# Layer 1's keys and values in one written order, between two layers of a fp32 transformer block on one core

## The chip, the cores and the metric

The kernel runs on one core of a Trainium2 chip. The metric is the device time of one execution in microseconds (us), the median of several runs; lower is better. A core has a matrix engine (TensorE, PE in the rows; its weight loads are shown apart as PEld), three engines for element-wise work (VectorE or DVE, ScalarE or ACT, GpSimd or POOL) and SyncE (SP), whose queue here issues the transfers between the core's memory and HBM. Each engine works through its own queue in order and waits on semaphores for the others.

## The reference

Two layers run over 1024 latent tokens and 256 context tokens of width 1024, all in fp32. Layer 0 is grouped-query attention, layer 1 multi-head latent attention. What the change touches lies at the border: layer 0's output projection with its gated residual, layer 1's norm and modulation, and layer 1's keys and values, which are made from a 256-wide compressed row and a 32-wide rotary key:

```python
x = x + gate[:, None, :] * y            # y = (o * silu(g)) @ w_out; likewise ctx with gate_c
h  = rms_norm(x, norm_w) * (1.0 + scale[:, None, :]) + shift[:, None, :]
hc = rms_norm(ctx, norm_w) * (1.0 + scale_c) + shift_c
...
kv = (rms_norm(kv_a, p["kv_a_norm"]) @ p["w_kv_b"]).reshape(B, n, MLA_HEADS, MLA_NOPE + MLA_V)
k_nope, v = jnp.split(kv, [MLA_NOPE], axis=-1)
return rms_norm(k_nope, p["k_nope_norm"]), rms_norm(k_r, p["k_rope_norm"]), v
```

## The kernel before, in words

Tokens come in ten tiles of 128 rows, tiles 0 to 7 latent and 8 and 9 context. A product of fp32 matrices is three matmuls per 128 rows of depth: each operand is split into a high part (a cast to a shorter format, ACT) and a low part (what is left, DVE or POOL), and `mm3` (lines 88 to 97) adds hi·hi, hi·lo and lo·hi in PSUM. Weights come from HBM into one of three buffers tagged `wraw` (`load_weight`, the cast in line 156, the subtraction in line 135), and the two parts go to a pair `wa`, `wb`, of which the ring has two. The raw rows of the attention's result (`oraw`) use the same three buffers.

At the end of layer 0, `out_proj` takes a tile at a time: the rows are split into `oh`, `ol`, 2 x 24 matmuls make `y` (the two halves of the output width use one weight pair each), DVE multiplies by the gate (`yt`), DVE and POOL add to the residual `xt`. `sink0` then stores latent tiles to `x1d` (a row of SP) and normalises `xt` in place: sum of squares on ACT (`junk`), mean on DVE, power of -1/2 on POOL (`x_rs`), scale on DVE (line 257). Since the scale writes in place, it has to wait until the store to `x1d` has read the tile. `modulate` turns a pair of normalised tiles by 16 transposes on PE (line 269), applies scale and shift (`hmod`, DVE), and splits into `hh` and `hl`. It is called one tile after the pair is complete; the context pair is modulated right behind `out_proj`.

Layer 1's keys and values are a software pipeline by `staged`: for a tile, compress (24 matmuls of 128x288, `mm`, lines 1280 to 1303), latent (3 transposes, split into `kvh` and `kvl`), expand (four groups of 6 matmuls of 128x512, `mmk` and `mmv`, for two halves of the heads; squares on ACT, `kss` and `kn_ms` on DVE, `kn_rs` on POOL, `kn` on DVE in line 1322; `v` copied out by ACT) and store (2 x 4 transposes of `kn`, `th` on ACT, `tl` on DVE, transfers). All products of this stage share four PSUM buffers. Only DVE is held to the written order there; the order of the other engines is chosen by the scheduler when the kernel is built. Then comes the q stage, whose compress step has 24 matmuls of 128x384 a tile.

Of the kernel before, what the change touches and what calls it, by code (L numbers as in the profile page):

```python
# [35 lines left out]
def hybrid_kernel(ctx: ExitStack, tc: tile.TileContext, ins: dict, out: bass.AP):  # L36
# [569 lines left out]
    def out_proj(l, ws, resid, sink, nt, op, xp, gp, ps_y, first, started, by_half):  # L606
# [24 lines left out]
        def mult(t, ks, first, last):  # L631
            oh, ol, xt, ys = t
            for n in range(2):
# [4 lines left out]
        def add(tt, t):  # L638
            oh, ol, xt, ys = t
            cond = 0 if tt < TL else 1  # L640
            for n in range(2):
                ns = slice(n * 512, (n + 1) * 512)
                yt = op.tile([P, 512], F32, name="yt", tag="yt")
# [550 lines left out]

    with ExitStack() as st:
        xp = st.enter_context(tc.tile_pool(name="xpp0", bufs=4, **right))
        gp = st.enter_context(tc.tile_pool(name="gp0", bufs=1, **right))
        wk = st.enter_context(tc.tile_pool(name="wk1a", bufs=3, **right))
# [14 lines left out]
        def sink0(tt, xt):  # L1213
# [17 lines left out]
        out_proj(0, wo, resid0, sink0, TT, op, xp, gp, ps_mm, first, started0, False)  # L1231
        stO.close()
        hT1.append(alloc_hT(stc, "hctx1", NC))
        flush(1)
# [11 lines left out]
    def bcast(tab, name, n):  # L1246
        t = tab.tile([P, n], F32, name="bc_" + name)
        sp.dma_start(t, ins[name].rearrange("(o d) -> o d", o=1).broadcast_to([P, n]))
        return t

    def rope_tables(tab):
        t = tab.tile([P, 2, TL, 32], F32, name="ropeB")
        sp.dma_start(t, ins["rope1"].rearrange("p (a t d) -> p a t d", a=2, t=TL))
        return t[:, 0], t[:, 1]

    stQ = ExitStack()
    qtab = stQ.enter_context(tc.tile_pool(name="tab1b", bufs=1, **right))
    w_qa = bcast(qtab, "l1_q_a_norm", 384)
    w_q = bcast(qtab, "l1_q_norm", 96)
    cosB, sinB = rope_tables(qtab)  # L1260
    pad(qtab, 128)
    with ExitStack() as st:
        tab = st.enter_context(tc.tile_pool(name="tab1a", bufs=1, **right))
        pad(tab, 96)
        wk = st.enter_context(tc.tile_pool(name="wk1b", bufs=6, **right))
        sg2 = st.enter_context(tc.tile_pool(name="stg1a", bufs=2, **right))
        latp = st.enter_context(tc.tile_pool(name="latp1a", bufs=4, **right))
        small = st.enter_context(tc.tile_pool(name="sml1b", bufs=3, **right))

        w_kva = bcast(tab, "l1_kv_a_norm", 256)  # L1270
        w_kr = bcast(tab, "l1_k_rope_norm", 32)
        w_kn = tab.tile([P, 1], F32, name="w_kn")
        for j in range(2):
            sp.dma_start(w_kn[64 * j:64 * j + 64, :], ins["l1_k_nope_norm"].rearrange("(d o) -> d o", o=1))
        wkvr = load_weight(w_in1, KT, 0, 288)
        wkvb = load_weight(ins["l1_w_kv_b"], 2, 0, 2048, 1)
        wkv_v = [w.rearrange("p k (h c d) -> p k h c d", c=2, d=64) for w in wkvb]

        def kv_compress(tt, _):
            ps = proj1(tt, wkvr, 288)  # L1280
            ss = small.tile([P, 2], F32, name="kvss", tag="kvss")
            sq = wk.tile([P, 512], F32, name="sq", tag="w512")
# [317 lines left out]
```

## Time and profile before

| | before |
|---|---|
| median of 3 runs (lowest to highest) | 1746.25 us (1745.01 to 1748.26) |
| the profiled execution: its time, its span | 1745.03 us, 1743.2 us |
| busy share of the span: PE, PEld, DVE, ACT, POOL | 98%, 71%, 61%, 37%, 56% |
| mean granted TensorE clock | 0.996 |
| output projection of layer 0 on PE, from the first `y` | 769.3 to 887.4 us |
| layer 1's keys and values on PE, up to the first matmul of the q stage | 887.4 to 999.1 us |

Times of the trace count from the start of the span. The profiled execution is 1.2 us below the median and has 1.83 us outside its span. The shares are means over stages with different limits.

### The profile page before, as it was taken

Reading aid. Unit: us, or ns where it says so; the run is one execution under the profiler, and the core shown is the slowest. Engines: PE = TensorE matmul, PEld = TensorE weight load, DVE = VectorE, ACT = ScalarE, POOL = GpSimd, SP = SyncE. Lnnn points to the kernel's source line nnn. Section 1 sums busy time; section 2 is a strip of 40 time slices with the busy share of each in tenths; the row PEclk is TensorE's granted clock in tenths of the full one; section 3 lists DMA queues with packets and bytes.
Section 4 is the critical chain, followed back from the end, with each engine's and each line's share of the span. In section 5 each row is a group of like instructions: output and inputs, shape, how many; then the busy total and the mean of one; then the engine's idle time right before and its main releaser. Section 6 shows DMA issues by size and latency. Waiting matters only on the chain. (4 is left out here: it accounts for less than half of the span.)

```text
span 1743.2 us, 23751 instructions
## 1 busy us (share of the span) xinstructions
PE 1706.6 (98%) x8524; PEld 1230.9 (71%) x8524; DVE 1064.4 (61%) x1803; ACT 644.5 (37%) x943; POOL 981.7 (56%) x659
## 2 busy tenths in 40 slices
PE   8899999999999999999989999999999999999998
PEld 5676778776555655558878798977566666666587
DVE  3664652368778877725675657756676767666231
ACT  4642221124444544432244633332343434334310
POOL 2763430237889798753344644443577878777511
PEclk9999999999999999999999999999999999999999
DMA  9457855431332422146434857685335443441352
GB/s 318 161 147 237 253 171 150 136 97 43 96 103 70 106 79 72 46 130 202 136 93 128 239 164 199 181 233 161 93 88 128 106 103 92 108 110 47 117 162 73
DMA packets 211757, 234.33 MB, mean 134 GB/s; under 512 B 20664, under 2 KB 157608, under 8 KB 211640
## 3 DMA queue, kind: packets, MB, share of 16 engines
q1 hardware_dynamic: 211216, 232.71, 46.8%
q8 instruction: 67, 1.10, 0.3%
q14 instruction: 50, 0.41, 0.1%
q10 hardware_dynamic: 424, 0.11, 0.0%
HBM read 158.98 MB, written 73.63 MB: 133 GB/s over the span
## 5 line engine op out<-in xcount | busy, mean ns | idle before, releaser
L362 DVE TENSOR_REDUCE m<-mx 128x1 f32<-128x512 f32 x512 | 351.4, 691 | 208.7 <-PE mx L361 206.3
L423 ACT ACTIVATE p<-st 128x1024 f32<-128x1024 f32 x328 | 335.1, 1025 | 223.0 <-PE st L421 192.1
L444 POOL TENSOR_TENSOR acp<-acp,p 128x1024 f32<-128x1024 f32 x128 | 305.6, 2387 | 8.7
L457 PE MATMUL av<-p,v 128*64 128x512 f32 x1312 | 289.9, 595 | 0.0
L457 PEld LDWEIGHTS av<-p,v 128*64 128x64 f32 x1312 | 90.8, 137 | 181.1 <-issue 178.7
L444 POOL TENSOR_TENSOR acp<-p 128x1024 f32<-128x1024 f32 x34 | 81.4, 2394 | 172.7 <-ACT p L423 172.3
L444 POOL TENSOR_TENSOR acp<-acp,acd 128x1024 f32<-128x1024 f32 x60 | 141.6, 2361 | 21.7 <-DVE acd L430 19.1
L430 DVE TENSOR_REDUCE acd<-p 128x512 f32<-128x1024 f32 x124 | 144.7, 1220 | 7.7 <-ACT p L423 7.7
L135 POOL TENSOR_TENSOR wb<-wraw,wa 128x512 fp32r<-128x512 f32 (+3 forms) x73 | 95.3, 1323 | 89.7 <-ACT wa L156 89.3
L92 PE MATMUL mm<-wa,hh 128*128 128x512 f32 (+2 forms) x336 | 127.3, 379 | 1.0 <-ACT hh L784 1.0
L94 PE MATMUL mm<-wa,hl 128*128 128x512 f32 (+2 forms) x336 | 121.8, 363 | 3.7 <-DVE hl L787 3.2
L421 PE MATMUL st<-QH,KL 96*128 96x512 f32 x320 | 123.1, 392 | 0.0
L93 PE MATMUL mm<-wb,hh 128*128 128x512 f32 (+2 forms) x336 | 121.1, 360 | 0.0
L478 ACT COPY os<-av 128x512 f32<-128x512 f32 x36 | 21.1, 586 | 252.9 <-PE av L457 156.5
L92 PE MATMUL y<-wa,oh 128*128 128x512 f32 x288 | 112.6, 391 | 0.0
L368 DVE TENSOR_REDUCE m<-mx 128x2 f32<-128x512 f32 x144 | 99.2, 692 | 22.0 <-PE mx L366 21.2
L93 PE MATMUL y<-wb,oh 128*128 128x512 f32 x288 | 112.2, 390 | 0.0
L94 PE MATMUL y<-wa,ol 128*128 128x512 f32 x288 | 112.1, 389 | 0.0
L421 PE MATMUL st<-QA,KA 128*128 128x512 f32 x336 | 106.6, 398 | 0.9 <-ACT p L423 0.9
L421 PE MATMUL st<-QB,KB 65*128 65x512 f32 x336 | 105.8, 395 | 0.0
L361 PE MATMUL mx<-KA,QA 128*128 128x512 f32 x256 | 102.3, 405 | 1.5 <-DMA KA<-k0l 0.8
L361 PE MATMUL mx<-KH,QH 96*128 96x512 f32 x256 | 102.4, 403 | 0.9 <-DVE m L362 0.7
(225 smaller groups left out, 3416.7 us busy)
## 6 DMA issues: line engine op xcount, KB each, us to landing
mraw<-in_l_w_mod SPq DMA_DIRECT2D x64, 256.0 KB
wraw<-in_l_w_in SPq DMA_DIRECT2D x28, 512.0 KB
rb<-rrow SPq DMA_DIRECT2D x72, 128.0 KB
mraw<-in_l_w_mod SPq DMA_DIRECT2D x16, 512.0 KB
sgd<-gth SPq DMA_DIRECT2D x32, 256.0 KB
QA<-q0h SPq DMA_DIRECT2D x32, 256.0 KB
wraw<-in_l_w_out SPq DMA_DIRECT2D x16, 512.0 KB
sg<-sgd SPq DMA_DIRECT2D x64, 128.0 KB
```

The lines of the kernel that those rows point to most:

```text
L92: pe.matmul(ps, lhsT=lh(k), rhs=rh(k), start=first and i == 0, stop=False)
L93: pe.matmul(ps, lhsT=lh(k), rhs=rl(k), start=False, stop=False)
L94: pe.matmul(ps, lhsT=ll(k), rhs=rh(k), start=False, stop=last and i == len(ks) - 1)
L135: eng.tensor_sub(lo, a, b)
L361: pe.matmul(m, lhsT=s["mq"][:, i * P:(i + 1) * P], rhs=s["mk"][:, n * 512:(n + 1) * 512], start=True, stop=True)
L362: dve.reduce_max(s["m"][:, i, n:n + 1], m, axis=AX.X)
L368: dve.reduce_max(s["m"][:, 2 * i:2 * i + 2, 2 if u["kind"] == "lat" else 0], m.rearrange("p (a b) -> p a b", a=2), axis=AX.X)
L421: pe.matmul(ps[:, n * 512:(n + 1) * 512], lhsT=lh, rhs=rf(n), start=(j == 0), stop=(j == len(prods) - 1))
L423: act.activation(p, ps, AF.Exp, scale=self.ops["scale"])
L430: dve.reduce_sum(t[:, ns], p2.rearrange("p a n -> p n a")[:, ns, :], axis=AX.X)
L444: pool.tensor_add(t, a, b)
L457: pe.matmul(s["av"][64 * n:64 * n + 64, :], lhsT=s["v"][:, kt, u["vc"]:u["vc"] + 64], rhs=p[:, n * 512:(n + 1) * 512], start=kt == kts[0], ...
```

## The change

Four edits go together.

1. **`out_proj` of layer 0.** For the two context tiles the products are ordered by halves of the weights: first half of tile 8, first half of tile 9, second half of tile 8, second half of tile 9. The context tiles' residual gets a pool of its own (`xcp`, 2 buffers); the pool of the latent ones goes from 4 buffers to 3, and two work pools get one buffer less.
2. **Context modulated late.** The context pair isn't modulated behind `out_proj` but in four groups of four transposes, in the second to fifth period of the key-value stage.
3. **Keys and values in one written order.** `staged` is replaced by a `Plan`: each step is entered with a time, the entries are sorted, and all five engines keep that order. Three compress steps come first, then a period of 10 for each tile. The q weights are loaded in the plan, and the first compress step of the q stage stands between the two halves of tile 9's expand.
4. **Tables.** Seven transfers of norm weights and the rope table become two (`gains1` 128x768, `rope1` 128x513), issued when tile 3's sink is written in `out_proj`.

```diff
@@ out_proj
-            xt = xp.tile([P, D], F32, name="xt", tag="xt")
+            xt = xp(tt).tile([P, D], F32, name="xt", tag="xt")
...
-        def mult(t, ks, first, last):
+        def mult(t, ks, first, last, halves=(0, 1)):
             oh, ol, xt, ys = t
-            for n in range(2):
+            for n in halves:
...
+        pair = {}
         for tt in range(together, nt):
...
             load_x(tt, t)
+            if nt > TL and tt >= TL:
+
+                pair[tt] = t
+                mult(t, range(KT), True, True, (0,))
+                continue
             mult(t, range(KT), True, True)
+            add(tt, t)
+        for tt, t in pair.items():
+            mult(t, range(KT), True, True, (1,))
             add(tt, t)
@@ around the call of out_proj
+    stQ, stK = ExitStack(), ExitStack()
+    qtab = stQ.enter_context(tc.tile_pool(name="tab1b", bufs=1, **right))
+    xcp = stK.enter_context(tc.tile_pool(name="xc1", bufs=2, **right))
+    gains1 = qtab.tile([P, 768], F32, name="gains1")
+    rope1 = qtab.tile([P, 2 * TL * 32 + 1], F32, name="rope1")
...
+    def tables1():
+        sp.dma_start(gains1, ins["gains1"].broadcast_to([P, 768]))
+        sp.dma_start(rope1, ins["rope1"])
...
-        xp = st.enter_context(tc.tile_pool(name="xpp0", bufs=4, **right))
+        xp = st.enter_context(tc.tile_pool(name="xpp0", bufs=3, **right))
...
+            if tt == 3:
+                tables1()
             if tt % 2 == 0:
                 flush(1)
-            else:
+            elif tt < TL:
                 hold.append((tt // 2, xs_of[tt // 2]))
...
         hT1.append(alloc_hT(stc, "hctx1", NC))
-        flush(1)
@@ keys and values of layer 1
+        weight1(wkvr, w_in1, KT, 0, 288, range(3), -20, (-5, -4, -3))
+        weight1(wkvb, ins["l1_w_kv_b"], 2, 0, 2048, (0, 2, 1, 3), -2.9, (1.5, 5, 8.7, 10.35), 1)
...
+        def group(k2):
+            modulate(1, 4, xs_of[4], hT, ps_tp, wk, 2, (k2,))
+
+        for k2, b in enumerate((25.5, 35.5, 45.5, 55.5)):
+            plan.at(b, group, k2)
...
+            plan.at(b, mult)
+            plan.at(b + 3.3, squares)
+            plan.at(b + 4.4, power)
+            plan.at(b + 5.2, gains)
...
+            plan.at(b, mult, 0)
+            plan.at(b + 1.36, mult, 1)
+            plan.at(b + 1.4, squares)
+            plan.at(b + 2.1, power)
+            plan.at(b + 2.8, values)
+            plan.at(b + 4.4, scale)
...
-        with in_order(mybir.EngineType.DVE):
-            staged(range(TT), kv_compress, kv_latent, later, later, kv_expand, kv_store)
...
+        for p_ in range(TT + 3):
+            b = (0, 3.3, 6.6)[p_] if p_ < 3 else 10 * p_ - 12
+            if p_ < TT:
+                sts[p_] = compress(p_, b)
+            if 0 <= p_ - 1 < TT:
+                latent(p_ - 1, sts[p_ - 1], (9.9, 11.2)[p_ - 1] if p_ < 3 else b + 3.3)
+            for g2 in range(2):
+                if 0 <= p_ - 2 < TT:
+                    expand(p_ - 2, sts[p_ - 2], g2, b + (5 if p_ < 3 else 3.7) + 3.2 * g2)
+                if 0 <= p_ - 3 < TT:
+                    store(p_ - 3, sts[p_ - 3], g2, b + 6.4 + 3.2 * g2)
...
+        weight1(wqa, w_in1, KT, 288, 384, range(4), 81.3, (82.5, 85.2, 88.5, 91.5))
+        q_first(0, 104.5)
+        plan.run()
```

How the order of instructions moves is shown at three places. In the names, the numbers count the tiles of the program and differ between the two kernels; what they are is said here.

**PE, from the last product of `out_proj` into the key-value stage.** Before: `y_7745` is the second half of tile 9, `xt_7629` the normalised tile 8 (of tile 9, `xt_7743`, the other 12 transposes follow 33 matmuls later), `mm_7940` tile 0's compress step.

```order
L94 MATMUL y_7745<-wa_3503,ol_7742 128x512
L269 MATMUL tp_7819<-ident_70,xt_7629 128x128
L269 MATMUL tp_7829<-ident_70,xt_7629 128x128
L269 MATMUL tp_7839<-ident_70,xt_7629 128x128
L269 MATMUL tp_7849<-ident_70,xt_7629 128x128
L92 MATMUL mm_7940<-wa_7896,hh_6931 128x288
L93 MATMUL mm_7940<-wb_7897,hh_6931 128x288
L94 MATMUL mm_7940<-wa_7896,hl_6932 128x288
```

Now, after `y_7678` (second half of tile 9), `mm_7882` (tile 0's compress step) follows at once:

```order
L93 MATMUL y_7678<-wb_3504,oh_7674 128x512
L94 MATMUL y_7678<-wa_3503,ol_7675 128x512
L92 MATMUL mm_7882<-wa_7848,hh_6940 128x288
L93 MATMUL mm_7882<-wb_7849,hh_6940 128x288
L94 MATMUL mm_7882<-wa_7848,hl_6941 128x288
```

Further on PE, behind the third compress step (`mm_7958`), stand the transposes of the compressed tiles 0 and 1 (`kvn`) and tile 0's expand (`mmk_8038`):

```order
L94 MATMUL mm_7958<-wa_7848,hl_6941 128x288
L1353 MATMUL tp_8003<-ident_70,kvn_7945 128x128 x2
L1354 MATMUL tp_8003<-ident_70,kvn_7945 32x128
L1353 MATMUL tp_8024<-ident_70,kvn_7988 128x128 x2
L1354 MATMUL tp_8024<-ident_70,kvn_7988 32x128
L92 MATMUL mmk_8038<-wa_7872,kvh_8007 128x512
L93 MATMUL mmk_8038<-wb_7873,kvh_8007 128x512
```

The transposes of the context tiles have left this place, and the expand of tile 0 comes after three compress steps where it came after five.

**SP, the transfers in the first tiles of `out_proj`.** Before: `oraw_7187` is tile 3, `xt_7184` tile 3's residual, `x1d<-xt_6893` and `x1d<-xt_6898` the stores of tiles 0 and 1.

```order
L597 DMA oraw_7187<-od0_97 128x8x128
L623 DMA xt_7184<-in_x 128x1024
L597 DMA oraw_7260<-od0_97 128x8x128
L597 DMA oraw_7373<-od0_97 128x8x128
L1215 DMA x1d_79<-xt_6893 128x1024
L597 DMA oraw_7446<-od0_97 128x8x128
L1215 DMA x1d_79<-xt_6898 128x1024
L597 DMA oraw_7559<-od0_97 128x8x128
```

Now: `oraw_7196` is tile 3, `xt_7640` and `xt_7676` are the residuals of the context tiles, `xt_6902` and `xt_6907` tiles 0 and 1.

```order
L597 DMA oraw_7196<-od0_97 128x8x128
L1213 DMA gains1_6881<-in_gains1 128x768
L1214 DMA rope1_6882<-in_rope1 128x513
L597 DMA oraw_7271<-od0_97 128x8x128
L597 DMA oraw_7384<-od0_97 128x8x128
L623 DMA xt_7640<-in_ctx 128x1024
L623 DMA xt_7676<-in_ctx 128x1024
L1236 DMA x1d_79<-xt_6902 128x1024
L597 DMA oraw_7457<-od0_97 128x8x128
L597 DMA oraw_7570<-od0_97 128x8x128
L1236 DMA x1d_79<-xt_6907 128x1024
L623 DMA xt_7193<-in_x 128x1024
```

The tables and the context residuals stand ahead of the stores of tiles 0 and 1, tile 7's `oraw` (`oraw_7570`) ahead of tile 1's store, and tile 3's residual (`xt_7193`) behind it.

**ACT, around the first expand.** Before: squares of tiles 3 and 4, the splits of tiles 0 to 3, and tile 0's first square of an expanded half (`sq_8225`).

```order
L85 CAST krh_8034<-tp_8026 32x128
L85 CAST kvh_8087<-tp_8083 128x256
L1283 ACTIVATE sq_8123,kvss_8122<-mm_8097 128x256
L1284 ACTIVATE sq_8123,kvss_8122<-mm_8097 128x32
L85 CAST krh_8091<-tp_8083 32x128
L85 CAST kvh_8144<-tp_8140 128x256
L85 CAST krh_8148<-tp_8140 32x128
L1283 ACTIVATE sq_8180,kvss_8179<-mm_8154 128x256
L1284 ACTIVATE sq_8180,kvss_8179<-mm_8154 128x32
L85 CAST kvh_8201<-tp_8197 128x256
L1337 ACTIVATE sq_8225<-mmk_8211 128x512
```

Now: the squares of tile 2, the split of tile 0, the fourth piece of `w_kv_b`, the split of tile 1, and tile 0's first square (`sq_8061`).

```order
L156 CAST wa_7872<-wraw_7878 128x1024
L1313 ACTIVATE sq_8000,kvss_7999<-mm_7958 128x256
L1314 ACTIVATE sq_8000,kvss_7999<-mm_7958 128x32
L85 CAST kvh_8007<-tp_8003 128x256
L85 CAST krh_8011<-tp_8003 32x128
L156 CAST wa_7872<-wraw_7880 128x1024
L85 CAST kvh_8028<-tp_8024 128x256
L85 CAST krh_8032<-tp_8024 32x128
L1383 ACTIVATE sq_8061<-mmk_8038 128x512
L1392 COPY v1_8069<-mmkv_8054 128x512
```

One cast of a weight piece and one more split stand between tile 0's split and the square of its first expanded half; this order can no longer change on its own.

## Rows read from the trace of the kernel before

**Rows 1.** The page, part 1: busy us (share of the span) xinstructions

```profile
PE 1706.6 (98%) x8524; PEld 1230.9 (71%) x8524; DVE 1064.4 (61%) x1803; ACT 644.5 (37%) x943; POOL 981.7 (56%) x659
```

**Rows 2.** Stretches: PE, PEld, DVE, ACT, POOL busy us; clock, DMA share, GB/s

```profile
890.00:900.00 10.00, 4.72 (x29) 4.49 (x29) 6.06 (x10) 5.52 (x7) 0.55 (x1) 0.73 0.71 226
900.00:910.00 10.00, 9.59 (x69) 9.13 (x68) 7.23 (x19) 4.49 (x18) 5.63 (x12) 0.93 0.51 142
910.00:920.00 10.00, 9.43 (x56) 7.97 (x56) 5.16 (x21) 4.63 (x17) 5.62 (x16) 1.00 0.06 13
930.00:940.00 10.00, 10.00 (x63) 8.96 (x62) 5.88 (x17) 4.80 (x13) 4.85 (x8) 1.00 0.56 161
...
990.00:1000.00 10.00, 7.79 (x41) 5.99 (x39) 6.04 (x12) 6.74 (x11) 6.43 (x4) 1.00 0.98 289
1000.00:1010.00 10.00, 9.71 (x49) 9.74 (x50) 5.20 (x7) 3.37 (x6) 5.63 (x3) 0.83 0.95 271
```

**Rows 3.** Waits of TensorE, 760 to 1060 us: total, times, longest

```profile
PE tp L269 <- DVE xt L257: 5.9, 2, 5.3
PE tp L1358 <- DVE kn L1322: 2.5, 2, 1.7
```

**Rows 4.** TensorE timeline, 887 to 898: start, us, instruction [idle before <-releaser]

```profile
888.10 0.29 PE L94 MATMUL mm<-wa,hl 128*128 128x288 f32 x1
888.23 0.29 PE L92 MATMUL mm<-wa,hh 128*128 128x288 f32 x1
...
897.62 2.82 PE L269 MATMUL tp<-ident,xt 128*128 128x128 f32 x12 [5.28 <-DVE xt L257]
```

**Rows 5.** Timeline of ScalarE, 883 to 896

```profile
883.49 2.77 ACT L156 CAST wa<-wraw 128x288 fp32r<-128x288 f32 x8
891.79 1.05 ACT L156 CAST wa<-wraw 128x1024 fp32r<-128x1024 f32 x1 [5.53 <-DMA wraw<-in_l_w_kv_b]
...
894.66 1.05 ACT L255 ACTIVATE junk<-xt 128x1024 bf16<-128x1024 f32 x1
```

**Rows 6.** Timeline of VectorE, 896 to 898

```profile
896.81 0.75 DVE L257 TENSOR_SCALAR xt<-xt,x_rs 128x1024 f32<-128x1024 f32 x1 [0.73 <-POOL x_rs L118]
```

**Rows 7.** Timeline of SyncE queue, 883 to 895

```profile
887.75 6.70 SPq L152 DMA_DIRECT2D wraw<-in_l_w_kv_b  x4
```

**Rows 8.** Timeline of TensorE, 995 to 1002

```profile
995.95 1.03 PE L1358 MATMUL tp<-ident,kn 128*128 128x128 f32 x8
998.69 0.63 PE L1358 MATMUL tp<-ident,kn 128*128 128x128 f32 x4 [1.71 <-DVE kn L1322]
...
1000.29 1.06 PE L1358 MATMUL tp<-ident,kn 128*128 128x128 f32 x4 [0.80 <-DVE kn L1322]
```

**Rows 9.** Groups of instructions, 920 to 980: busy us, mean ns | idle

```profile
L118 POOL TENSOR_TENSOR kn_rs<-kn_ms,mhalf 128x8 f32<-128x8 f32 x14 | 23.2, 1661 | 10.7 <-DVE kn_ms L116 10.7
...
L1322 DVE TENSOR_TENSOR kn<-mmk,kn_rs 128x512 f32<-128x512 f32 x13 | 8.9, 688 | 8.5 <-POOL kn_rs L118 8.5
L1339 DVE TENSOR_REDUCE kss<-sq 128x8 f32<-128x512 f32 x13 | 8.8, 674 | 5.7 <-ACT sq L1337 5.7
L1337 ACT ACTIVATE sq<-mmk 128x512 f32<-128x512 f32 x14 | 8.4, 599 | 7.3 <-PE mmk L94 7.3
```

**Rows 10.** Timeline of SyncE queue, 799 to 802

```profile
799.85 0.33 SPq L1215 DMA_DIRECT2D x1d<-xt  x1
801.00 0.36 SPq L597 DMA_DIRECT2D oraw<-od  x1
```

**Rows 11.** Timeline of VectorE, 802 to 804

```profile
802.94 1.23 DVE L257 TENSOR_SCALAR xt<-xt,x_rs 128x1024 f32<-128x1024 f32 x1 [0.69 <-DMA x1d<-xt]
```

**Rows 12.** Timeline of TensorE, 804 to 806

```profile
804.22 1.86 PE L269 MATMUL tp<-ident,xt 128*128 128x128 f32 x15 [0.64 <-DVE xt L257]
```

**Rows 13.** Busy time by stretch, out_proj of layer 0

```profile
795.00:800.00 5.00, 5.00 (x24) 4.14 (x23) 2.10 (x4) 2.14 (x4) 0.79 (x2) 1.00 1.15 329
800.00:805.00 5.00, 4.36 (x24) 3.46 (x23) 4.27 (x7) 2.16 (x3) 2.05 (x3) 1.00 0.74 228
```

More of the change, by code (lines that the diff above doesn't have):

```diff
@@ L1321, in scale_k @@
[L1321 to L1337 removed]
+        plan = Plan()
@@ new lines, in weight1, with alloc @@
+        def weight1(slot, w, kt, c0, cols, order, begin, splits, share=2):
+            pieces, held = [], {}
+            def alloc():
+                slot.extend(load_weight(w, kt, c0, cols, share, todo=pieces))
+            plan.at(begin, alloc)
+            for n, i in enumerate(order):
+                plan.at(begin + 0.01 * n, lambda i=i: held.update({i: pieces[i]()}))
+                plan.at(splits[n], lambda i=i: held[i]())
+        wkvr, wkvb, wqa = [], [], []
+        weight1(wkvr, w_in1, KT, 0, 288, range(3), -20, (-5, -4, -3))
@@ new lines, in latent, with turn, parts @@
+        def latent(tt, st, b):
+            cs = slice(tt * P, (tt + 1) * P)
+            def turn():
+                kn = st["kn"]
+                st["tp"] = tp = ps_tp.tile([P, 512], F32, name="tp", tag="tp")
+                for j in range(2):
+                    pe.transpose(tp[:, j * P:(j + 1) * P], kn[:, j * P:(j + 1) * P], ident)
+                pe.transpose(tp[:32, 256:384], kn[:, 256:288], ident)
+            def parts():
+                tp = st["tp"]
+                st["kvh"] = latp.tile([P, 2, P], F32R, name="kvh", tag="lat_h")
+                st["kvl"] = latp.tile([P, 2, P], F32R, name="kvl", tag="lat_l")
+                split(st["kvh"], st["kvl"], tp[:, :256].rearrange("p (a n) -> p a n", a=2))
+                a = small.tile([32, P], F32R, name="krh", tag="krh", bufs=1)
+                b = small.tile([32, P], F32R, name="krl", tag="krl", bufs=1)
+                split(a, b, tp[:32, 256:384])
+                sp.dma_start(kr1h[:, cs], raw(a))
+                sp.dma_start(kr1l[:, cs], raw(b))
+            plan.at(b, turn)
+            plan.at(b + 0.4, parts)
@@ new lines, in expand, with mult, squares, power @@
+        def expand(tt, st, g2, b):
+            hs = slice(8 * g2, 8 * g2 + 8)
+            g = st[g2] = {}
+            def mult(c):
+                kvh, kvl = st["kvh"], st["kvl"]
+                wh, wl = (w.rearrange("p k (h c d) -> p k h c d", c=2, d=64) for w in wkvb)
+                g[c] = ps_mm.tile([P, 512], F32, name="mmkv"[:3 + c], tag="mm")
+                mm3(g[c], lambda k: kvh[:, k, :], lambda k: kvl[:, k, :],
+                    lambda k: wh[:, k, hs, c, :], lambda k: wl[:, k, hs, c, :], range(2))
+            def squares():
+                g["sq"] = wk.tile([P, 512], F32, name="sq", tag="w512")
+                act.activation(g["sq"], g[0], AF.Square)
+            def power():
@@ L1353, in kv_store, with store, turn @@
+            plan.at(b, mult, 0)
[4 more added lines that the diff above has]
+            plan.at(b + 4.4, scale)
+        def store(tt, st, g2, b):
             cs = slice(tt * P, (tt + 1) * P)
-            for g2 in range(2):
-                kn = held[g2]
-                tp = ps_tp.tile([P, 512], F32, name="tp", tag="tp")
+            g = st[g2]
+            def turn():
+                g["tp"] = ps_tp.tile([P, 512], F32, name="tp", tag="tp")
```

179 lines of the change are left out of this document (80 added, 99 removed).

## The prediction

> **What bounds the kernel now.** I read the page's busy shares first: TensorE works 98% of the span, the others 37% to 61% [rows 1]. So a change can win only where PE waits or runs at a lower clock, and only in the stretch in which the order moves, from layer 0's output projection to the start of the q stage. The reader should therefore go next to the stretches. In the middle of the key-value stage PE is busy 10.00 of 10 us, while DVE, ACT and POOL are busy 4.80 to 5.88: nothing is to be had there, and each helper has about half its time free. At the start (890 to 920) and at the end (990 to 1010) it is otherwise [rows 2]. The view of waits names the two causes: transposes of line 269 wait 5.9 us for the scaled tile `xt`, transposes of line 1358 wait 2.5 us for `kn` [rows 3].
>
> The timeline shows how the long wait comes about. The 12 context transposes start at 897.62 after 5.28 us of idle PE [rows 4]. Tile 9 needs a sum of squares (`junk`), and ACT does it only at 894.66, behind two weight casts; ACT itself waited 5.53 us for the first of these weights [rows 5]. Their transfers were issued from 887.75 on [rows 7], because the three raw buffers were still held by the split of the layer's first weights (casts from 883.49 [rows 5]). The scale follows at 896.81 [rows 6].
>
> **Term 1, the start of the stage: gain 8.2.** PE's idle time is 5.28, 0.41 and 0.57 us in the three stretches from 890 to 920. [...] Sum 6.26 + 1.9 = 8.2. The change takes the cause away: the context transposes leave this place, the compress weights can be split about two half products (some 11 us) earlier, since the ring's first pair is free when tile 9's first half is done, and ACT's wait has nothing of PE behind it. The 16 late transposes cost PE the same wherever they stand; ACT, DVE and POOL do their casts and scales in the half-free periods.
>
> **Term 2, the end: gain 3.9.** Two waits of 1.71 and 0.80 us for `kn` [rows 8] are all of the idle time in 990 to 1010 (2.21 + 0.29), and the clock of 0.83 in the second stretch costs (1 - 0.83) x 10 = 1.7 us [rows 2]. Together 4.2. The chain behind the last `mmk` is square 0.60, sum 0.67, power 1.66, scale 0.69 [rows 9], 3.6 us, and a small mean step on DVE. Now one group of six matmuls, eight transposes and 14 matmuls of the second q tile cover it. From starts 0.13 us apart for 288 columns [rows 4] I estimate 0.23 for 512 columns and 0.17 for 384: 6 x 0.23 + 14 x 0.17 = 3.8, and 1.03 for eight transposes [rows 8], 4.8 us in all. I keep 0.3 for queues.
>
> **Term 3, new waits while the pipeline fills: loss 2.5, and 0.8 for the clock.** Tile 0's expand now comes after three compress steps, not five, and every engine keeps its order. On ACT, `kvh` of tile 0 waits behind tile 2's squares, while before more compress steps covered it: about 0.8 us, bounded by nothing and one square of 0.6 and a split. Tile 3's compress step needs the PSUM buffer that tile 0's first `mmk` leaves, so the scale of `kn` must be done. Chain 3.6 us; cover is three groups of 1.4, 4.2 us. In the chain, though, a weight cast of 1.05 [rows 5] and a split on ACT, and a subtraction on DVE about as long as the cast, stand ahead. If both count, PE waits 3.6 + 1.05 + 1.05 + about 0.4 - 4.2 = 1.9 us; if the queues slip past each other, nothing. I take 1.7, nearer to the upper end as the order is fixed: 0.8 + 1.7 = 2.5 (0 to 2.7). After two waits of 1.71 and 0.80 the clock fell and cost 1.7; after one of 0.64 [rows 12] it stayed at 1.00 [rows 13]. A wait of 1.7 lies between: I take 0.8 (0 to 1.7).
>
> **Term 4, transfers in `out_proj`: loss 2.7, and 0.8 for the clock.** The transposes of the first pair already wait 0.64 us [rows 12], since the scale of tile 1 waits until its store has read the tile [rows 11]. That store is issued at 799.85, and tile 7's `oraw` at 801.00 [rows 10]. Now this `oraw` stands ahead of the store, and it waits for its raw buffer until 801.00, so the store can't be issued before about 801.4: 1.5 us later. Ahead stand also 0.66 MB of tables (128 x 768 and 128 x 513 words) and 1.05 MB of context residuals; tile 3's residual (0.52 MB) went behind. The sum is 1.18 MB more, at the 329 GB/s of a stretch whose DMA share is 1.15 [rows 13] 3.6 us. So the wait grows by 1.5 (the late issue alone) to 3.6 (queues full throughout); the share falls to 0.74 from 800 on, so part is absorbed: 2.7. The lower end is nothing, if PE itself arrives later: it may, since the first tile's `oh` now is cast behind the last copies of the attention result; a delay there is not added, as both end in the same wait. The clock again 0.8 (0 to 1.7).
>
> [...]
>
> **What costs nothing.** The seven old tables were issued in the fill, and no wait for them is in the view [rows 3]; two transfers save SP's time only, which nobody waits for. The q weights are cast about 13 us of the plan ahead of their use, in periods where ACT is half free [rows 2]; without that cover each late piece costs a cast and a subtraction, about 2 us. Smaller pools (3 residuals, 2 `yt`) make loads wait, but a tile takes 11 us of PE and a load of 0.52 MB 1.6.
>
> **Sum.** Gain 8.2 + 3.9 = 12.1; loss 2.5 + 0.8 + 2.7 + 0.8 = 6.8; net -5.3 us. The profiled execution of 1745.03 (span 1743.2 and 1.83 around it) becomes 1739.7; it lies 1.2 below the median, so the median of 1746.25 becomes 1740.9.
>
> **Rivals.**
> - **All covered, 1734.** The queues are short, the transfers fit: losses nothing, net -12.1. For it: helpers half free [rows 2]. Against it: the queue on SP is longer by count.
> - **Given back, 1744.** Losses at their upper ends: 2.7 + 1.7 + 3.6 + 1.7 = 9.7, net -2.4. For it: the first pair's wait exists already [rows 12]. Measured, that is no change: this kernel's runs spread 3.3 us, and 0.2% (3.5 us) is about what a measurement can tell.
> - **Slower, 1750.** In each of seven periods the next compress step needs the PSUM buffer of the `mmk` before. The cover is 3 x 1.4 + 1.0 = 5.2 us against a chain of 3.6, a slack of 1.6. All engines now keep one order, so a `kn_rs` of 1.66 [rows 9] behind another one and behind one more subtraction of about 1.3 adds 3.0, and PE waits 1.4 a period, 9.8 us in all: 1740.9 + 9.8 = 1750.7. It decides from (5.3 + 3.5)/7 = 1.3 us of wait a period. Against it: half-free helpers.
>
> **Numbers.** Forecast 0.43, all covered 0.24, given back 0.20, slower 0.13. Faster by over 0.2% (below 1742.8): 0.43 x 0.95 + 0.24 = 0.65; within: 0.20 + 0.43 x 0.05 = 0.22; slower: 0.13. The range reaches from all covered, 1733, to 1748, and leaves out what lies beyond. The forecast's own range is 1736 to 1743.
>
> **What would show it.** After: no wait of line 269 near 887 to 900 and clock 1.00 there; the `kn` wait at the end below 0.5; a wait of about 2 us before tile 3's compress step; the first pair's transposes in `out_proj` waiting about 3 us for `xt`, with `x1d` as cause of the late scale. It is wrong if PE shows waits in every period of the stage, or if the q stage waits for weights.

## The result, and the profile after

The changed kernel takes 1750.51 us (median of 15 runs, 1747.28 to 1756.59) against 1746.66 us (15 runs, 1744.59 to 1749.30) for the kernel before. The ratio is 1.0022, 95% interval 1.0015 to 1.0030: slower by 3.9 us where 5.3 us less was forecast, and outside the range.

The profiled execution has a span of 1749.5 us, 6.3 us more than that of before. To see where, I cut both traces where TensorE starts the same work, and take the starts from its timeline: the last scores of layer 0's attention (766.11 us before, 767.86 after), the first product of the output projection (769.31, 772.86), the instruction behind its last product (887.40, 897.68), the instruction behind the eighth q tile's compress step (1037.20, 1040.43), the first scores of layer 1's attention (1202.79, 1209.22) and the last instruction (1738.20, 1744.63). The differences are the lengths:

| stretch of TensorE, us | before | after | change |
|---|---|---|---|
| to the last scores of layer 0 | 766.11 | 767.86 | +1.75 |
| A: from there to the first `y` | 3.20 | 5.00 | +1.8 |
| B: output projection | 118.09 | 124.82 | +6.7 |
| C: keys and values, and eight q tiles | 149.81 | 142.75 | -7.1 |
| D: rest of the q stage to the first scores | 165.59 | 168.79 | +3.2 |
| layer 1's attention to the end | 535.41 | 535.41 | 0 |

The first row isn't put down to the change. TensorE's instructions in it are the same in both kernels (on ACT and VectorE, two casts of `oh` and two subtractions of `ol` have moved out of it), and in the traces below it is 763.6 to 769.3 us without order. A to D give +4.7 us, the median +3.9. C splits further at the start of the second q tile: up to there 118.94 before and 109.08 after (-9.9), the seven tiles from there 30.87 and 33.67 (+2.8).

So the part at which the change aims did what was forecast, and what was lost lies around it. The stretches of the changed kernel show the same, with columns as in [rows 2]:

```profile
770.00:780.00 10.00, 8.78 (x50) 5.73 (x47) 2.74 (x5) 2.27 (x3) 2.58 (x2) 1.00 0.53 168
...
800.00:810.00 10.00, 7.20 (x32) 5.52 (x30) 4.42 (x8) 4.30 (x6) 3.29 (x3) 1.00 1.07 344
810.00:820.00 10.00, 8.16 (x32) 7.18 (x33) 7.39 (x14) 2.80 (x5) 2.80 (x2) 0.66 0.40 121
...
890.00:900.00 10.00, 10.00 (x61) 8.90 (x60) 9.19 (x15) 3.17 (x6) 3.80 (x4) 1.00 0.35 122
900.00:910.00 10.00, 8.42 (x61) 7.58 (x59) 7.43 (x16) 6.24 (x19) 5.65 (x11) 1.00 0.16 55
910.00:920.00 10.00, 9.03 (x53) 8.00 (x53) 5.82 (x15) 3.92 (x9) 5.02 (x9) 1.00 0.19 60
990.00:1000.00 10.00, 9.58 (x48) 7.23 (x47) 7.48 (x15) 5.78 (x13) 6.34 (x6) 1.00 0.84 241
1000.00:1010.00 10.00, 9.99 (x59) 9.14 (x58) 5.70 (x12) 2.83 (x6) 4.83 (x4) 1.00 0.65 186
1030.00:1050.00 20.00, 18.22 (x111) 17.81 (x110) 13.78 (x40) 6.25 (x17) 10.68 (x16) 1.00 0.41 116
1050.00:1070.00 20.00, 17.05 (x98) 16.54 (x97) 16.04 (x42) 9.12 (x19) 9.16 (x11) 0.91 0.66 180
```

The reader is to see four things. From 890 to 920 PE is idle 2.55 us (0, 1.58 and 0.97) at a clock of 1.00, where it was idle 6.26 us with a clock down to 0.73 [rows 2]. From 990 to 1010 it is idle 0.43 us and the clock stays up, against 2.5 us and 0.83. But from 770 to 820 it is idle 5.9 us (1.22, 2.80 and 1.84), and the clock in the last of these stretches is 0.66; before there was one wait of 0.64 us [rows 12, 13]. And from 1030 to 1070 it is idle 4.7 us, against 1.4.

The waits of TensorE in the changed kernel, from 760 to 1110 us (total, times, longest):

```profile
PE tp L269 <- DVE xt L257: 4.3, 1, 4.3
PE tp L1590 <- DVE tl L86: 3.0, 1, 3.0
PE mm L92 <- DVE qa_ms L116: 1.8, 1, 1.8
PE tp L1353 <- DVE kvn L1328: 1.2, 1, 1.2
PE tp L1354 <- POOL kvn L1338: 1.1, 1, 1.1
PE av L499 <- ACT os L478: 0.7, 1, 0.7
PE y L94 <- DVE ol L629: 0.5, 1, 0.5
...
PE mmkv L92 <- DVE kn L1397: 0.3, 1, 0.3
PE tp L1353 <- DVE kvms L1320: 0.2, 1, 0.2
```

The 5.3 us wait of line 269 at the stage's start is gone [rows 3], and the largest wait is now one of line 269 again, of 4.3 us, in the output projection. The wait for `kn` (2.5 us before) is down to 0.3. Two waits of the q stage are new or longer: 1.8 us behind VectorE's `qa_ms`, and 3.0 us in line 1590, where the kernel before has 1.4.

What makes the 4.3 us shows on two queues. The transfers that SP issues, in the changed kernel:

```profile
792.17 0.63 SPq L1213 DMA_DIRECT2D gains<-in_gains  x1
792.85 0.42 SPq L1214 DMA_DIRECT2D rope<-in_rope  x1
793.38 2.14 SPq L597 DMA_DIRECT2D oraw<-od  x2
795.57 3.41 SPq L623 DMA_DIRECT2D xt<-in_ctx  x2
799.09 0.36 SPq L1236 DMA_DIRECT2D x1d<-xt  x1
800.54 4.08 SPq L597 DMA_DIRECT2D oraw<-od  x2
804.85 1.35 SPq L1236 DMA_DIRECT2D x1d<-xt  x1
```

VectorE in the same stretch:

```profile
802.89 0.15 DVE L116 TENSOR_SCALAR x_ms<-xss 128x1 f32<-128x1 f32 x1 [1.78 <-ACT junk L255]
802.96 1.22 DVE L629 TENSOR_TENSOR ol<-oraw,oh 128x1024 fp32r<-128x1024 f32 x1
804.10 0.69 DVE L645 TENSOR_TENSOR xt<-xt,yt 128x512 f32<-128x512 f32 x1
...
811.03 0.75 DVE L257 TENSOR_SCALAR xt<-xt,x_rs 128x1024 f32<-128x1024 f32 x1 [3.26 <-DMA x1d<-xt]
```

In the kernel before, VectorE had:

```profile
799.02 0.15 DVE L116 TENSOR_SCALAR x_ms<-xss 128x1 f32<-128x1 f32 x1 [2.90 <-ACT junk L255]
799.10 0.69 DVE L645 TENSOR_TENSOR xt<-xt,yt 128x512 f32<-128x512 f32 x1
799.71 1.22 DVE L629 TENSOR_TENSOR ol<-oraw,oh 128x1024 fp32r<-128x1024 f32 x1
```

The tables (`gains`, `rope`) go out at 792.2, the context residuals from 795.6 on, and each takes its turn in front of what the first tiles need. `x_ms` waits for tile 0's `junk` on ACT; `ol` of tile 4 follows it at once, and the add of tile 1 (804.10), which came ahead of `ol` before, now stands behind it. Tile 1's store can't be issued before that add is done, so it goes out at 804.85 (799.85 before [rows 10]), behind tile 7's `oraw` on SP, and the tile is free only at 811.03, when the scale starts (802.94 before [rows 11]).

These times can't be compared as they stand, since the changed kernel comes to its first product 3.5 us later (1.75 of the first row and 1.8 of A). Counted from the first product (769.31 and 772.86), tile 0's `x_ms` is 0.3 us later than before, the add and the issue of the store 1.45 us later (31.99 against 30.54), and the scale 4.5 us later (38.17 against 33.63). So the store is issued 1.45 us later and then takes 6.2 us where it took 3.1. The DMA share from 800 to 810 is 1.07; from 800 to 805 it was 0.74 [rows 13].

### The profile page after: what moved, and what is told of

Same layout as the page of the kernel before. It is cut to its first block, busy times and chain, and to the rows that moved or that the text cites. A ratio compares the mean times of both kernels' runs of the same rounds, so it can differ in the third digit from the quotient of the medians.

```text
span 1749.5 us, 23739 instructions
## 1 busy us (share of the span) xinstructions
PE 1710.9 (98%) x8524; PEld 1233.6 (71%) x8524; DVE 1064.9 (61%) x1803; ACT 642.3 (37%) x943; POOL 985.2 (56%) x659
## 4 chain that ended last, share of the span: by engine, by line
PE 78%; DVE 7%; DMA 5%; POOL 4%; issue 3%; ACT 1%; SPq 0%; POOLq 0%; DVEq 0%; ACTq 0%
PE st L421 19%; PE av L457 15%; PE mm L92 7%; PE mm L94 6%; PE mx L361 6%; PE mm L93 6%; PE y L92 3%; PE y L93 3%; PE y L94 3%; DVE m L362 2%; PE mx L366 2%; PE av L499 1%; PE pm L199 1%; DVE m L368 1%; DMA xt<-in_x 1%
```

## The experiments

Each kernel was profiled and timed beside the kernel before. The table at the end of this section has the stretches of all; the trace is of one execution each, the time the median of several. The edits are to the changed kernel unless the text says otherwise.

**1. Tables and context residuals held back.** One column of each destination is copied from a value that is made later (tile 3's normalised residual, tile 8's `oh`), so that the transfers have to wait; the copied column is then overwritten. The edit:

```diff
+            if nt > TL and tt >= TL:
+                pool.tensor_copy(t[2][:, :1], raw(t[0][:, 0, :1]))
             sp.dma_start(t[2], resid(tt))
...
+        for t in (gains1, rope1):
+            pool.tensor_copy(t[:, :1], xt[:, :1])
```

What is looked at is TensorE's wait for tile 1's scale, 4.3 us in the changed kernel, and the clock granted behind it, 0.50 from 812 to 816 us.

> The changed kernel, but the two table transfers and the two context residuals can start only after work of later tiles (one column of each destination is first copied from a normalised tile 3 or from tile 8's oh), so on SP they come behind the stores of tiles 0 and 1. [...] Theory A (the transfers put ahead delay oraw, the add of tile 1 and its store): that wait falls below 1.5 us, the clock stays up, the output projection ends 5 to 7 us earlier, and the run takes about 1745. Rival B (the late start of the first products and the smaller pools make the wait): the wait stays above 3 us and the time stays within 1.5 us of the changed kernel's 1750.5.

Measured: 1748.66 us (1.0020 of before, 1.0009 to 1.0030). B is 119.46 us in the trace, 5.4 less, but the wait for tile 1's scale is still 2.4 us. Theory A's 5 to 7 us are there, but not its wait and not its time: beside the changed kernel's 1.0022 the time hardly moves, so something else is left.

**2. q weights as before.** No weights of the q stage and no q step in the plan:

```diff
-        weight1(wqa, w_in1, KT, 288, 384, range(4), 81.3, (82.5, 85.2, 88.5, 91.5))
-        q_first(0, 104.5)
...
+        wqa = load_weight(w_in1, KT, 288, 384)
```

> The changed kernel, but the q weights are loaded where they were before and no q compress step stands in the plan. In the changed kernel the stretch from the second q tile to the first score of layer 1's attention took 6 us longer than before. Theory A (in the plan the first pieces of w_q_b and the gate weights are issued some 14 us later, and their splits collide with the q stage): that stretch gets 4 to 6 us shorter, the end of the key-value stage loses 0 to 4, and the run takes 1745 to 1750. Rival B (the stretch is longer for another cause, such as the tables' or pools' new places): the stretch stays within 1 us of the changed kernel's.

Measured: 1751.63 us (1.0028, 1.0013 to 1.0043). The seven q tiles take 30.87 us as before, and the whole way from the second q tile to the first scores is 4.4 us shorter, which is theory A's 4 to 6. But the key-value stage up to the second q tile takes 113.78 us, 4.7 more than with the early q step, so nothing is won, and the time lies above theory A's.

**3. q weights in the plan, no q step.**

```diff
-        q_first(0, 104.5)
```

> The changed kernel with the q weights in the plan as they are, but without the q compress step there, so no raw buffer is held by its result. If the held buffer is what makes w_q_b late, the stretch after the second q tile gets 3 us or more shorter; if it is that the q weights themselves are written late in the plan, it stays within 1.5 us of the changed kernel's.

Measured: 1752.41 us (1.0043, 1.0028 to 1.0058; 4 runs). The seven q tiles are at 30.87 us again: it is the q step or what it holds, not when the q weights are written. Experiment 10 separates the two. The stage up to the second q tile takes 115.12.

**4. Experiments 1 and 2 together.**

> The edits of the first two runs together. If both theories A hold, the gains add up: output projection 5 to 7 us and q stage 4 to 6 less what the end of the key-value stage loses, so about 1740 to 1743, faster than the kernel before. If both rivals hold, 1749 to 1751.

Measured: 1748.35 us (1.0018, 1.0009 to 1.0027). They don't add up. B is 122.83 with a wait of 3.8 us, though every engine has the same order there as in experiment 1 (119.46, 2.4). The remaining wait thus varies from one execution to the next by more than I had assumed, and one profile can't size it. In the changed kernel's own output projection it varies less: that kernel and experiments 2, 3 and 10 have the same order on every engine, and there the wait is 4.3 us each time and B 123.9 to 124.9.

**5. `oh` in its old place as well.** The pool of `oh` and `ol` is opened ahead of two small pools, so that tile 0's `oh` doesn't lie on the last tiles of the attention:

```diff
+        op = st.enter_context(tc.tile_pool(name="opp0", bufs=3, **right))
         wk = st.enter_context(tc.tile_pool(name="wk1a", bufs=2, **right))
         small = st.enter_context(tc.tile_pool(name="sml1a", bufs=3, **right))
         pad(small, 224)
-        stO = ExitStack()
-        op = stO.enter_context(tc.tile_pool(name="opp0", bufs=3, **right))
```

> The changed kernel with tables and context residuals held back as in the first experiment, and with the pool of oh and ol opened ahead of two small pools, so that tile 0's oh no longer lies on the last tiles of the attention. On ACT the casts of oh stand ahead of the last copies again, as in the kernel before. Theory A (two separate losses in the output projection, the transfers put ahead and the late first product): from the last score to the first product 3.2 us as before, not 5.0; the wait for tile 1's scale below 1.5 us; the output projection 118 to 120 us; the run 2 to 5 us below the kernel before, 1741 to 1744. Rival (the start doesn't matter since the wait for the store absorbs it): output projection plus start as long as in the first experiment, 1746 to 1749.

Measured: 1748.22 us (1.0012, 1.0003 to 1.0022). A is 3.20 us as before, but the wait for the scale is 2.9 us and B 121.93. Theory A is missed in wait, B and time: there is a third cause. A and B together are 125.1 us, 124.5 in experiment 1, and the time lies in the rival's range: beside experiment 1 the 1.8 us of the earlier start seem to end in the wait.

**6. The written order alone.** The output projection, the context's modulation and the pools are those of the kernel before; the plan, the early q step and the two table transfers (now at the start of the stage) stay. Beside the first two parts of the change's diff, the edit undoes:

```diff
-        for k2, b in enumerate((25.5, 35.5, 45.5, 55.5)):
-            plan.at(b, group, k2)
...
         hT1.append(alloc_hT(stc, "hctx1", NC))
+        flush(1)
```

> The kernel before with the written order of keys and values alone (its q compress step and two table transfers included, at the start of the stage): output projection, context modulation and pools are those of the kernel before. Theory A: start 3.2 and output projection 118 us as before; the wait of about 5 us for the last context tile returns at the start of the stage, the end and the q stage are those of the changed kernel, so 1746 to 1750. Rival (the loss is in the written order itself): slower than the changed kernel, above 1751.

Measured: 1748.56 us (1.0016, 1.0006 to 1.0026). A and B are 3.20 and 117.65, as before, and a wait of 4.9 us for the context tile is back. Theory A holds: the loss before 890 belongs to the changed output projection. The written order alone makes the stage up to the second q tile 3.4 us shorter (115.51 against 118.94), but the seven q tiles take 34.64, 3.8 more, so it doesn't win without the late context.

**7. `oh` in its old place, nothing else** (the diff of experiment 5 alone).

> The changed kernel with only the pool of oh and ol opened earlier, tables and context residuals as in the change. Theory A: the start is 3.2 us again, but the store of tile 1 is still behind the same transfers, so PE arrives earlier and waits longer: output projection 125 to 127 us, time within 1 us of the changed kernel. Rival (the late start causes the late transfers): the whole loss of 8.5 us goes, about 1742.

Measured: 1747.98 us (1.0010, 0.9998 to 1.0023). A falls by 1.8 us and B to 122.94, with a wait of 2.6 us. Neither theory is met, but the edit has moved something else too. SP's queue in this kernel:

```profile
802.55 0.32 SPq L1235 DMA_DIRECT2D x1d<-xt  x1
802.98 0.37 SPq L597 DMA_DIRECT2D oraw<-od  x1
```

Tile 1's store now stands ahead of tile 7's rows, as in experiment 12, and it takes 4.5 us as there (4.4), not 6.2. So the shorter wait can't be put down to `oh`. Beside experiment 12, A is 1.8 us shorter and B 1.1 longer.

**8. Tables alone held back** (the second half of experiment 1's diff).

> The changed kernel with only the two tables held back (0.66 MB), context residuals (1.05 MB) as in the change. If each byte ahead of tile 1's store counts alike, about 0.4 of what the first experiment recovered in the output projection (5.4 us) comes back, some 2 us; if only what stands ahead of the fifth and sixth oraw counts, the tables are the larger part, 3 us or more.

Measured: 1746.10 us (1.0001, 0.9992 to 1.0011). B is 122.03, 2.8 us less, between the two expectations, and no more than experiments 1 and 4 differ by, so it doesn't decide between them; the wait is 3.1 us. The time is 2.6 us below that of experiment 1, which holds back more; no run explains that.

**9. Tile 1's store ahead of tile 7's rows, on top of experiment 5.**

```diff
+            if nt > TL and tt == TL - 1:
+                pool.tensor_copy(r[:, :1], ready[1][2][:, :1])
             fetch_o(l, tt, r, slice(0, KT))
```

> The fifth kernel (tables and context residuals held back, oh in its old place) with one more hold: tile 7's oraw is fetched only after one column of its buffer has been copied from tile 1's normalised residual, so that on SP it stands behind tile 1's store, as in the kernel before. In the fifth run the transposes of the first pair still waited 2.9 us. Theory A (what is left of the wait is this order on SP): the wait falls below 1.2 us and the output projection to 118 to 119.5 us. Rival (it is the later load of tile 3's residual or DVE's order): the wait stays above 2 us.

Measured: 1743.09 us (0.9986, 0.9977 to 0.9995), the first kernel faster than before. No wait for `xt` of 0.3 us or more is left, and B is 118.49. SP's queue in this kernel, where `x1d` at 801.13 is tile 1's store:

```profile
798.59 0.36 SPq L597 DMA_DIRECT2D oraw<-od  x1
801.13 0.33 SPq L1241 DMA_DIRECT2D x1d<-xt  x1
805.37 0.36 SPq L597 DMA_DIRECT2D oraw<-od  x1
```

VectorE, tile 1's add and scale:

```profile
800.37 0.69 DVE L647 TENSOR_TENSOR xt<-xt,yt 128x512 f32<-128x512 f32 x1
...
803.88 1.15 DVE L257 TENSOR_SCALAR xt<-xt,x_rs 128x1024 f32<-128x1024 f32 x1 [0.78 <-DMA x1d<-xt]
```

The add is done at 801.1, the store is issued at once, and the scale follows 2.8 us behind it (6.2 in the changed kernel, 6.1 in experiment 5). Up to the end of the output projection every engine's order is otherwise that of experiment 5, so the store's shorter way comes from this one place on SP: theory A. The smaller pools are in this kernel too, and its B is within 0.4 us of the kernel before.

**10. The early q result outside the raw buffers.** It is put into columns of the gains table that are no longer read, and 96 new ones:

```diff
-                done_q[tt] = qn = rawp.tile([P, 1024], F32, name="qan", tag="wraw")[:, :384]
+                done_q[tt] = qn = gains1[:, 480:864]
```

> The changed kernel, but the result of the early q compress step lies in columns of the gains table that are no longer needed, and a little more, not in one of the three raw weight buffers. On SP the second and third piece of w_q_b then stand 7 rows earlier. Theory A (the held raw buffer makes the weights of the q stage late): the seven q tiles from the second to the last take 30.9 us as in the kernel before, not 33.7, with the gain at the end of the key-value stage kept; the run 2 to 4 us below the changed kernel's. Rival (it is the q step itself that shifts the splits): 33 us or more.

Measured: 1747.61 us (1.0015, 1.0005 to 1.0024). The seven q tiles take 31.60 us, 2.1 of the 2.8 are back, and the stage up to the second keeps its gain (109.15). By the ratios the run is 1.2 us below the changed kernel, less than forecast and not clear of noise. Two rows each of SP's queue show what moved, the first pieces of `w_q_b` and of the gate weights (`in_l_w_in`). In the kernel before:

```profile
969.79 0.41 SPq L152 DMA_DIRECT2D wraw<-in_l_w_q_b  x1
...
1002.43 0.68 SPq L152 DMA_DIRECT2D wraw<-in_l_w_in  x1
```

In the changed kernel:

```profile
1009.72 0.51 SPq L152 DMA_DIRECT2D wraw<-in_l_w_q_b  x1
...
1016.83 0.38 SPq L152 DMA_DIRECT2D wraw<-in_l_w_in  x1
```

In this experiment:

```profile
991.60 1.67 SPq L152 DMA_DIRECT2D wraw<-in_l_w_q_b  x1
...
1014.62 2.88 SPq L152 DMA_DIRECT2D wraw<-in_l_w_in  x3
```

All three start the first q tile's products at 998 to 999 us, so these times can be compared: `w_q_b` starts at 969.8, 1009.7 and 991.6, the gate weights at 1002.4, 1016.8 and 1014.6. Where they are late, their subtractions land in the middle of the q steps (the last one on VectorE at 1018.8, 1030.5 and 1027.1). VectorE in the changed kernel:

```profile
1030.54 0.69 DVE L135 TENSOR_TENSOR wb<-wraw,wa 128x512 fp32r<-128x512 f32 x1 [1.01 <-ACT wa L156]
1031.14 1.65 DVE L1580 TENSOR_TENSOR t<-t,q_rs 128x384 f32<-128x384 f32 x1
```

It stands 1.0 us for a weight cast, and the scale of `t` behind it takes 1.65 us (0.56 elsewhere), beside a gate subtraction on GpSimd from 1031.10 to 1032.38. PE's wait of 1.8 us follows at 1033.7. Experiments 1, 5, 7, 8, 9 and 12 have this wait too (1.2 to 2.2 us); this one, experiment 11 and those without an early q step (2, 3 and 4) don't.

**11. All four mends together** (experiments 5, 9 and 10).

> All mends together: tables and context residuals held back, oh in its old place, tile 1's store ahead of tile 7's oraw, the early q result outside the raw buffers. If the losses are these four and add, the run is the kernel before less the gain of the key-value stage with the q stage restored: 5 to 8 us below the kernel before, 1738 to 1741. If part of the loss is the written order itself, it ends at 1742 to 1746.

Measured: 1741.50 us (11 runs, 1736.41 to 1743.80) against 1745.56 us; ratio 0.9970, 0.9960 to 0.9980. It beats both kernels: 4 us below before, 9 below the changed one. The forecast of 1738 to 1741 is missed by half a microsecond. Its profile is shorter than that of before by 7.4 us over A to D, but the profiled execution is the shortest of the eleven, 5.1 us below their median; the medians give a little more than half of it. The waits that are left from 760 to 1110 us:

```profile
PE tp L1594 <- DVE tl L86: 3.0, 1, 3.0
PE tp L1357 <- DVE kvn L1332: 1.1, 1, 1.1
PE y L92 <- DVE yt L646: 1.1, 1, 1.1
PE tp L1358 <- POOL kvn L1342: 1.1, 1, 1.1
```

**12. The store's order on SP alone** (the diff of experiment 9 on the changed kernel).

> The changed kernel with only one hold: tile 7's oraw is fetched after a copy from tile 1's normalised residual, so that on SP it stands behind tile 1's store. Tables, context residuals and the place of oh stay as in the change. Theory A (bytes ahead of the store and the order on SP both count): the wait for tile 1's scale falls from 4.3 to between 1.5 and 3.5 us and the output projection to between 121 and 123.5 us. Rival 1 (the order on SP is all of it): wait below 1 us, output projection below 120. Rival 2 (the add of tile 1, late on DVE behind a late oraw, sets the store whatever stands on SP): wait above 3.5 us, output projection above 123.5.

Measured: 1746.39 us (1.0007, 0.9997 to 1.0017). The wait is 2.5 us and B 121.80: theory A, both count. Up to the end of the output projection every engine's order is otherwise that of the changed kernel; the store takes 4.4 us, not 6.2.

The stretches, worked out as above from one profile each; "wait" is the one for tile 1's scale, "store" the time from the issue of tile 1's store to that scale (in experiment 6 the scale waits for GpSimd's add instead), "q 2 to 8" is part of C, the ratio is to the kernel before in the same session. The profiled executions of 1, 7, 8, 9 and 11 are the shortest of their kernels and that of 12 the longest, so A to D and the ratios don't rank alike:

| kernel | A | B | wait | store | C | q 2 to 8 | D | A to D | ratio |
|---|---|---|---|---|---|---|---|---|---|
| before | 3.20 | 118.09 | 0.6 | 3.1 | 149.81 | 30.87 | 165.59 | 436.7 |  |
| changed | 5.00 | 124.82 | 4.3 | 6.2 | 142.75 | 33.67 | 168.79 | 441.4 | 1.0022 |
| 1 transfers held | 4.99 | 119.46 | 2.4 | 6.1 | 144.32 | 33.65 | 167.26 | 436.0 | 1.0020 |
| 2 q as before | 4.99 | 124.90 | 4.3 | 6.2 | 144.64 | 30.87 | 167.17 | 441.7 | 1.0028 |
| 3 no q step | 5.00 | 123.93 | 4.3 | 6.2 | 145.99 | 30.87 | 166.49 | 441.4 | 1.0043 |
| 4 = 1 + 2 | 4.99 | 122.83 | 3.8 | 7.0 | 146.09 | 30.87 | 168.22 | 442.1 | 1.0018 |
| 5 = 1 + `oh` | 3.20 | 121.93 | 2.9 | 6.1 | 144.95 | 35.70 | 166.82 | 436.9 | 1.0012 |
| 6 order alone | 3.20 | 117.65 | 0.2 |  | 150.15 | 34.64 | 167.91 | 438.9 | 1.0016 |
| 7 `oh` alone | 3.19 | 122.94 | 2.6 | 4.5 | 142.31 | 33.33 | 167.03 | 435.5 | 1.0010 |
| 8 tables held | 5.00 | 122.03 | 3.1 | 6.3 | 144.85 | 35.64 | 165.53 | 437.4 | 1.0001 |
| 9 = 5 + store first | 3.20 | 118.49 | 0 | 2.8 | 144.04 | 33.22 | 167.50 | 433.2 | 0.9986 |
| 10 q result moved | 5.00 | 124.06 | 4.3 | 6.2 | 140.74 | 31.60 | 166.88 | 436.7 | 1.0015 |
| 11 = 9 + 10 | 3.20 | 118.80 | 0 | 3.0 | 140.79 | 31.60 | 166.47 | 429.3 | 0.9970 |
| 12 store first alone | 5.00 | 121.80 | 2.5 | 4.4 | 144.83 | 34.18 | 169.09 | 440.7 | 1.0007 |

## Why the prediction was wrong

**Right: the stage itself.** Terms 1 to 3 were -8.2, -3.9 and +3.3, -8.8 together; up to the second q tile the stage is 9.9 us shorter. The end's wait fell to 0.3 as forecast. No run shows by itself the 1.9 us that term 1 sets for the clock. What the traces show is a clock of 0.73 and 0.93 from 890 to 910 in the kernel before [rows 2], where the compress products start 0.24 us apart from 900.48 to 900.96 and 0.13 apart from 901.40 to 901.66, and a clock of 1.00 in the changed kernel.

**Term 3, wrong in place, and near in size by chance.** The fill costs 2.4 us of waits (1.15, 1.10 and 0.17), but not at tile 3's compress step. PE waits for tile 1's `kvn`. VectorE in the changed kernel:

```profile
904.09 0.75 DVE L257 TENSOR_SCALAR xt<-xt,x_rs 128x1024 f32<-128x1024 f32 x1 [0.73 <-POOL x_rs L118]
904.76 0.15 DVE L1319 TENSOR_SCALAR kvms<-kvss 128x1 f32<-128x1 f32 x1
```

The mean of tile 0 (`kvms`) stands behind the scale of the last context tile, so the in-order chain of tiles 0 and 1 starts with the context's normalisation, which nobody waits for yet. The second of the waits ends when GpSimd is done with its part of `kvn`, behind a multiplication that took 1.23 us where 0.25 is usual (last section). This is read from the trace; no run moved it. The clock stayed at 1.00, so the 0.8 for it wasn't paid.

**Term 4, the step that failed.** Forecast was a loss of 2.7 and 0.8 for the clock in the output projection; measured are 6.7 in B and 1.8 in A. The mechanism was right, transfers put ahead of tile 1's store; the size was wrong in three places.

The first is the store. That it is issued 1.45 us later, counted from the first product, is what the term said (1.5), though VectorE's order has its part in it. But the term took the late issue and the longer way through the queues as the two ends of one range (1.5 to 3.6) and 2.7 between them. They add: 1.45 and 3.1 are the 4.5 us by which the scale is late. PE comes to it 0.4 us later itself, and the wait grows by 3.6. That this is the range's upper end is chance, since the sum behind that end leaves out tile 7's rows: they go ahead of the store as well, 0.52 MB, and with them it is 1.71 MB and, at the same 329 GB/s, 5.2 us. The runs tell the two parts of the delay apart. With tables, or tables and context residuals, held back and the start as in the change (experiments 1, 4 and 8), the store is issued 1.9 to 2.6 us earlier than in the changed kernel, but still takes 6.1 to 7.0 us. With nothing but tile 7's rows put behind it (12), it is issued only 0.2 us earlier, but takes 4.4. With both, and `oh` in its old place (9 and 11), it takes 2.8 and 3.0 us, about as before the change, and only then does the wait vanish.

The second is the clock, priced at 0.8, at most 1.7. After the 4.3 us wait PE ran at a granted clock of 0.50 and then 0.68 (stretches of 2 us in the changed kernel):

```profile
812.00:814.00 2.00, 2.00 (x10) 2.00 (x11) 1.61 (x4) 0.00 (x0) 0.00 (x0) 0.50 0.00 0
814.00:816.00 2.00, 2.00 (x10) 1.80 (x9) 2.00 (x5) 1.91 (x4) 0.49 (x1) 0.50 0.00 0
816.00:818.00 2.00, 2.00 (x8) 1.56 (x7) 1.16 (x2) 0.27 (x1) 2.00 (x2) 0.68 0.94 209
```

Counted as in term 2, as (1 - clock) x time, I estimate 0.50 x 4 + 0.32 x 2 = 2.6 us from these rows. The products of `y` start 0.42 to 0.43 us apart from 815.53 to 817.23, and 0.23 apart from 805.83 to 806.51, ahead of the wait. With 3.6 of wait and the 0.5 of the wait for `ol` this is B's 6.7.

The third is the late first product, said to end "in the same wait" and not added. The 0.5 us for `ol` come from it; they are gone in the kernels with `oh` in its old place (5, 7, 9 and 11), where a wait of 0.4 to 1.3 us for `yt` stands instead. Whether its 1.8 us in A add as well is open. In the changed kernel the rows are late together with the products (ACT casts tile 4's rows 27.6 us behind the first product before, 27.9 now), which speaks for it; experiment 5 beside experiment 1 speaks against it, and no run moves `oh` and leaves SP's order as in the change.

**"What costs nothing", the other step that failed.** It looked at the q weights' cover and not at what is queued behind them. The q step's result holds one of three raw buffers, so `w_q_b` and the gate weights are issued later and their splits collide with the q steps: 2.8 us in seven tiles, of which experiment 10 gives back 2.1, and experiments 2 and 3, without the q step, all. A q stage held up by its weights was one of the prediction's own signs of being wrong.

**Added up.** Between the forecast of -5.3 and the +4.7 of A to D lie some 10 us: 1.8 in A, 3.2 in B, 2.8 in the seven q tiles and 3.2 in D, less 1.1 that the stage gained beyond its forecast.

**The rivals.** Slower was forecast as one case, at 1750.7, with a chance of 0.13, and the time came near it by chance, by another mechanism: no period of the stage shows the wait for PSUM (PE busy 10.00 of 10 from 920 to 990). "Given back" put the loss on terms 3 and 4, with 5.3 for term 4, and left out the q stage.

**Open.** D, a third of the miss, is 165.53 to 169.09 in these profiles, and in experiment 8, whose edit is not in that part, it is as short as before; so its 3.2 us aren't shown to be the change's. The wait of line 1590 there is 1.4 us before and 3.0 after, also in the best kernel, and no run was aimed at it. Experiments 1 and 4 show that B can vary by 3 us with the same order there, so B of one profile is no better than that.

## What to carry to other kernels

When a change moves transfers ahead, look for the store or load behind them that some engine waits for, and add two things: how much later it is issued, and how much longer it then takes. Here the two had different causes: transfers far ahead made the issue late (it came 1.9 to 2.6 us earlier with them held back), and one transfer right ahead of the store made its way long (6.2 us, and 4.4 with the store ahead of it). Look also at what would be loaded next into a buffer that is kept one step longer: here it was paid for one stage later, with 2.1 us of the seven q tiles (experiment 10). And a plan that gains where it was aimed can still lose: cut both traces at the same instructions, and mend the neighbours before giving the plan up.

## What was not expected of the hardware

Behind the wait of 4.3 us before the transposes the granted clock was 0.50, 0.50 and 0.68 in stretches of 2 us (the three above), which I put at 2.6 us. Behind waits of 1.2 and 1.1 us at 909 to 911, one shortly after the other, it was 1.00 (910 to 920), where behind 1.71 and 0.80 it had been 0.83 [rows 2, 8].

A small operation of GpSimd took 1.23 us once, beside a subtraction of VectorE, and 0.25 or 0.26 us the other seven times. The same multiplication on 128x32 for tile 0 and for tile 1, in the changed kernel, and VectorE's subtraction beside the second:

```profile
907.38 0.25 POOL L1337 TENSOR_TENSOR krt<-kvn,rope 128x32 f32<-128x32 f32 x1
...
909.36 1.23 POOL L1337 TENSOR_TENSOR krt<-kvn,rope 128x32 f32<-128x32 f32 x1
```

```profile
909.23 1.25 DVE L135 TENSOR_TENSOR wb<-wraw,wa 128x1024 fp32r<-128x1024 f32 x1
```

The second multiplication starts 0.13 us behind the subtraction, and both end within 0.2 us of each other. What made it longer is not shown: no run moved either of the two.
